# Both split parts of an operand in one tile, at chosen byte places

## The chip, the cores and the metric

The program runs on one core of a Trainium2 chip. The metric is the device time of one execution in microseconds, taken as the median of several runs; of the kernel before, three runs took 3246.57, 3247.99 and 3251.56 us. The page and the trace come from one profiled execution.

## The reference

Two stacks of layers work on 256 tokens of 1024 channels, in float32. The first block has two layers, each with a feed-forward, an attention of three kinds of heads and another feed-forward, whose norms are modulated by a vector c. The second has four layers, each with a mixer (a state-space model in layers 0 and 3, gated linear attention in 1, a gated delta rule in 2), a cross-attention to 256 memory tokens and a convolved feed-forward. Nearly all arithmetic is products with weights:

```python
def swiglu(h, w1, w3, w2):
    return (jax.nn.silu(h @ w1) * (h @ w3)) @ w2
...
x = x + 0.5 * g1 * swiglu(h, ffn_w1[layer, 0], ffn_w3[layer, 0], ffn_w2[layer, 0])
...
for i in range(DEPTH_2):
    hn = rmsnorm_2(x, ln_mix[i])
    mix = ...                      # mamba2_mixer, hgrn2_mixer or gated_deltanet_mixer
    x = x + mix.astype(x.dtype)
    x = x + memory_cross_attention(rmsnorm_2(x, ln_xattn[i]), rmsnorm_2(mem, ln_mem[i]), ...)
    x = x + conv_glu_ffn(rmsnorm_2(x, ln_ffn[i]), f_up[i], f_conv_w[i], f_conv_b[i], f_down[i])
return rmsnorm_2(x, final_norm)
```

D_FF is 2816. Products must come out at float32 precision.

## The kernel before

Activations lie channels on partitions, tokens along the free dimension. Each product is made of 128x128 blocks of weights as the stationary operand (`lhsT`, loaded by LDWEIGHTS) and 256 tokens of an activation as the one that streams past them (`rhs`). In a few places the roles are swapped, and weights stream past an activation: `wide_half`, and the memory's values in `kv`.

For precision both operands are split into two float32r parts that add up to them. `split` (L244 to L247) makes the high part with a copy on ACT and the low part with a subtraction on DVE, or, for a quarter of some slabs, on POOL. `mm3` (L312) then issues three matmuls: high by high, high by low and low by high. So one block costs three loads of weights and three matmuls of 256 columns.

Weights come from HBM as slabs of 128 x 2048 floats, 1 MB each, by `slab` (L249): SP loads a slab into one of three staging tiles `w`, then ACT and DVE write its parts into tiles `wh` and `wl`, of which there are three each, in two to four pieces. A slab serves 48 matmuls. An up projection (`up_block`) takes 8 chunks of the contraction by 3 matmuls for each of a slab's two column blocks; a down projection (`down_step`) 8 column blocks by 3 matmuls for each of two chunks, into four PSUM banks `acc`. A feed-forward (`glu`) goes over 11 groups of two up slabs and one down slab, the down product one group behind.

Tile names: `hh`/`hl` are a normed input's parts, `eh`/`el` those of a modulated norm with two shift columns behind each chunk (258 columns), `mh`/`ml` the memory's, `gh`/`gl` a feed-forward's inner values, `oh`/`ol`, `xoh`/`xol`, `myh`/`myl`, `hyh`/`hyl`, `gyh`/`gyl` outputs of the heads, `xk`, `xq`, `xp`, `xv` cross-attention's keys, queries, probabilities and values. Names in rows are written output, arrow, then what is read.

A scheduler orders each engine's instructions from the traced order and from what becomes free, and the tile framework sets the addresses within a partition: tiles follow each other as they are allocated, each beginning at a multiple of 32 bytes. In the built program they begin as follows, in bytes past a multiple of 512:

| tiles | before | after: the part's first byte |
|---|---|---|
| wh, wl (all three slots) | 32 | 0 |
| hh, hl | 64 | 192 |
| gh, gl of the first block (four tiles each) | 224 | 192 |
| gh, gl of the second block (two each) | 64 | 192 |
| xoh, xol | 64 | 192 |
| myh, myl, hyh, hyl | 320 | 192 |
| oh, ol, gyh, gyl | 256 | 192 |
| mh, ml (the memory's: first three layers, last) | 192, 64 | 192 or 448 |
| xph, xpl | 320 | 192 |
| xvh, xvl | 64 | 0 |
| xkh, xkl (stream past xq) | 64 | 0 |
| xqh, xql | 64 | 64 |
| eh, el (chunks of 1032 bytes: first chunk) | 352, 416 | 352, 416 |

Every chunk and column block of the weights and of h, g, o, m, xo, my and hy is a whole multiple of 512 bytes on, so that these places hold for each matmul on them; those of e move on by 8 bytes a chunk.

Of the kernel before, what the change touches and what calls it, by code (L numbers as in the profile page):

```python
# [8 lines left out]
F32 = mybir.dt.float32  # L9
F32R = mybir.dt.float32r  # L10
BF16 = mybir.dt.bfloat16
AF = mybir.ActivationFunctionType
OP = mybir.AluOpType
# [3 lines left out]
P = 128  # L17
T = 256
# [8 lines left out]
# ---------------------------------------------------------------- layout of small vectors  # L27
# [8 lines left out]
NMEM = 32  # L36
COFF, NCOL = {}, 0
# [7 lines left out]
def _consts():  # L45
# [11 lines left out]
        # sums from after a chunk's middle to each token, or negative from after the token to the middle  # L57
# [12 lines left out]
def _prepare(i):  # L70
    """Lays the inputs out: weights as slabs in the order they are used, vectors as columns."""
# [15 lines left out]
    def up(w, order=None):  # L87
        """[.., 1024, n] -> [.., n / 256, 128, 8, 256], column blocks of 128 in the order given."""
        lead, n = w.shape[:-2], w.shape[-1]
        w = w.reshape(-1, KC, P, n // P, P)  # L90
        if order is not None:
            w = w[:, :, :, order]
        nb = w.shape[3]
        w = w.reshape(-1, KC, P, nb // 2, 2 * P).transpose(0, 3, 2, 1, 4)
        return np.ascontiguousarray(w).reshape(*lead, nb // 2, P, KC * 2 * P)

    def down(w):
        """[.., k, 1024] -> [.., k / 256, 128, 2, 1024]."""
# [4 lines left out]
    def wide(w):  # L103
        """[.., 1024, n] -> [.., 2, 128, 4, n]: halves of the contraction."""
# [4 lines left out]
    def flat(w):  # L109
        """[.., 1024, n] -> [.., 128, 8 * n]."""  # L110
# [62 lines left out]
# ---------------------------------------------------------------- the program  # L173


class Normed:
    """The parts of something to be normed, and each token's factor, once it is worked out."""
# [10 lines left out]
class Net:  # L188
# [19 lines left out]
    # ---- small helpers  # L208

    @contextmanager  # L210
    def phase(self, name):
        """Tiles of a part of the program, given back at its end."""
# [10 lines left out]
    def t(self, shape, tag, dtype=F32, bufs=None, pool=None):  # L223
        pool = pool or self.tp
        k = {} if bufs is None else {"bufs": bufs}
        return pool.tile(list(shape), dtype, tag=tag, name=self.name(tag), **k)

# [16 lines left out]
    def split(self, src, hi, lo, engine=None):  # L244
        """src as a sum of two parts; returns the two instructions."""
# [3 lines left out]
    def slab(self, src, n=2048):  # L249
        """A slab of weights, as two parts that add up to it exactly."""  # L250
# [6 lines left out]
        hi = self.t([P, 2048], "wh", F32R, pool=self.sp)[:, :n]  # L257
        lo = self.t([P, 2048], "wl", F32R, pool=self.sp)[:, :n]
        m = n // self.pieces
        for k in range(0, n, m):  # L260
# [6 lines left out]
            if self.slabs == 2:  # L267
                # this slab's place is in use until the norm's input is there
# [16 lines left out]
    def link(self, ins):  # L285
        """In a chain the tensor engine keeps to the order that is traced."""
# [10 lines left out]
    def mm3(self, out, a, b, start, stop):  # L297
        """out += a.T @ b, both given as exact sums of two parts."""
# [7 lines left out]
    def rsqrt(self, out, src, scale):  # L306
        """out = (src * scale + eps) ** -0.5"""
# [3 lines left out]
    def newton(self, r, src, scale, n):  # L311
        """One step of Newton's for r = (src * scale + eps) ** -0.5"""  # L312
# [8 lines left out]
    def after(self, ins, before):  # L321
        """Issues ins behind an earlier instruction of its engine."""
# [7 lines left out]
    def act(self, out, src, func, **k):  # L330
        """An activation of one of the two tables in use: Silu's, or the one with both Ln and Exp. The scalar
        engine takes turns with them as they are traced."""
# [11 lines left out]
    # ---- start  # L344

    def load_cols(self):
        """All vectors but the memory's gains."""
# [33 lines left out]
    def load_consts(self):  # L381
        """Tables, and masks made from them."""
# [11 lines left out]
        # biases: queries on partitions (keys after the query), keys on partitions (keys from the query on)  # L394
# [9 lines left out]
    def start(self, kv):  # L404
        """The first of the memory's keys and values go along with the first modulation."""
# [17 lines left out]
    # ---- modulation  # L423

    def ada_slab(self, l, s):
        """256 columns of layer l's modulation: rows of its weights, over partitions, with silu(c)."""
# [30 lines left out]
    def need(self, l, chunk):  # L457
        """Has columns [chunk * 1024, ..) of layer l's modulation worked out by now."""
# [3 lines left out]
    def mod_cols(self, l, i):  # L462
        """(gain, shift) of the i-th norm of layer l."""
# [19 lines left out]
    # ---- norms  # L483

    def square_sums(self, b, x, s, engine=None, behind=None):
        """Adds the squares of x's pair of chunks b to the sums so far; the last give what is left to add up."""
# [29 lines left out]
    def rstd(self, parts, cols=False, r=None):  # L516
        """Each token's reciprocal root mean square, on all partitions; with cols also over tokens, behind."""
# [12 lines left out]
    def parts_of(self, x, gain, eh, el, sums=True, beside=None):  # L530
        """The parts of x * gain; and the sums of x's squares, but for the last addition."""
# [18 lines left out]
    def norm(self, gain, cols=False):  # L550
        """x normed, as the parts of x * gain, and a factor for each token, which goes to what comes of
        products with them."""
        e = [self.t([P, KC, T], "h" + k, F32R, pool=self.hp) for k in "hl"]
        return Normed(self, e, self.parts_of(self.x, gain, *e), cols)

    def norm_shift(self, gain, shift):
        """x normed and shifted: h, its parts; and for products that need not wait for the root mean
        square: e, x normed, with the parts of the shift behind each chunk."""
# [7 lines left out]
        h = [self.t([P, KC, T], "h" + k, F32R, pool=self.hp) for k in "hl"]  # L566
# [23 lines left out]
    def scale(self, out, ps, r):  # L590
        """out [128, n, T] = products with e, of a bank or a part of it, times r."""
# [5 lines left out]
    def project(self, src, n, tag, bufs=2, bank=None):  # L597
        """Two blocks of a projection of x normed: [128, 2, T]."""
# [7 lines left out]
    # ---- feed forward  # L606
# [5 lines left out]
    def down_step(self, acc, w, j, g, first, last, banks=range(4)):  # L612
        """acc += w[k-chunk j].T @ g"""
# [1506 lines left out]
```

## Time and profile before

| | us |
|---|---|
| median of three runs | 3247.99 |
| lowest, highest | 3246.57, 3251.56 |
| the profiled execution's own span | 3242.8 |
| PE busy (matmuls) | 3123.4 (96%) |
| PEld busy (loads of weights) | 3022.4 (93%) |
| DVE busy | 2406.3 (74%) |
| ACT busy | 1874.0 (58%) |
| POOL busy | 614.6 (19%) |
| mean DMA rate | 193 GB/s, 624.85 MB in all |

The span goes from the first instruction to the last; a run's time has some launch and end around it, here 5.2 us between the span and the median. A matmul's listed duration reaches from its start to the modelled end of its result and overlaps the next ones, so that a matmul of 256 columns is shown with some 280 ns although the next begins long before; the pace of a run of matmuls is read from their starts. The granted clock of TensorE is 0.989 of full speed on the mean.

### The profile page before, as it was taken

Reading aid. Unit: us, or ns where it says so; the run is one execution under the profiler, and the core shown is the slowest. Engines: PE = TensorE matmul, PEld = TensorE weight load, DVE = VectorE, ACT = ScalarE, POOL = GpSimd, SP = SyncE. Lnnn points to the kernel's source line nnn. Section 1 sums busy time; section 2 is a strip of 40 time slices with the busy share of each in tenths; the row PEclk is TensorE's granted clock in tenths of the full one; section 3 lists DMA queues with packets and bytes.
Section 4 is the critical chain, followed back from the end, with each engine's and each line's share of the span. In section 5 each row is a group of like instructions: output and inputs, shape, how many; then the busy total and the mean of one; then the engine's idle time right before and its main releaser. Section 6 shows DMA issues by size and latency. Waiting matters only on the chain. (4 is left out here: it accounts for less than half of the span.)

```text
span 3242.8 us, 63167 instructions
## 1 busy us (share of the span) xinstructions
PE 3123.4 (96%) x25866; PEld 3022.4 (93%) x25866; DVE 2406.3 (74%) x4122; ACT 1874.0 (58%) x3317; POOL 614.6 (19%) x522
## 2 busy tenths in 40 slices
PE   8999999999999999999999999998899999999998
PEld 8999889999988999889999999997799999889998
DVE  6877778777776857887767677688857766887765
ACT  5544566454466546775546655476466545776544
POOL 1100232010032102433001220036422000443100
PEclk9999999999999999999999999999999999999999
DMA  8978436758843655444554445544334555545453
GB/s 286 320 292 312 175 125 216 292 216 298 303 171 120 220 185 187 164 163 170 182 186 155 142 169 173 191 163 157 130 118 156 198 196 186 176 163 184 162 188 118
DMA packets 96754, 624.85 MB, mean 193 GB/s; under 512 B 10640, under 2 KB 14800, under 8 KB 25424
## 3 DMA queue, kind: packets, MB, share of 16 engines
q1 hardware_dynamic: 96464, 620.82, 54.7%
q8 instruction: 203, 3.33, 0.4%
q14 instruction: 87, 0.71, 0.1%
HBM read 607.08 MB, written 13.70 MB: 191 GB/s over the span
## 5 line engine op out<-in xcount | busy, mean ns | idle before, releaser
L246 ACT ACTIVATE wh<-w 128x512 fp32r<-128x512 f32 (+3 forms) x1392 | 1034.7, 788 | 773.7 <-issue 251.0
L247 DVE TENSOR_TENSOR wl<-w,wh 128x512 fp32r<-128x512 f32 (+3 forms) x1195 | 1140.9, 982 | 370.9 <-ACT wh L246 367.3
L283 PE MATMUL up<-hh,wh 128*128 128x256 f32 x4120 | 1158.2, 283 | 6.6 <-DVE gpr L593 6.2
L283 PE MATMUL up<-hh,wl 128*128 128x256 f32 x4120 | 1148.5, 281 | 1.3 <-DVE wl L247 1.0
L283 PE MATMUL up<-hl,wh 128*128 128x256 f32 x4120 | 1133.2, 282 | 4.1 <-DVE hl L247 4.1
L283 PEld LDWEIGHTS up<-hh,wh 128*128 128x128 f32 x4120 | 781.2, 190 | 15.9 <-ACT wh L246 7.0
L283 PEld LDWEIGHTS up<-hh,wl 128*128 128x128 f32 x4120 | 781.1, 190 | 2.6 <-DVE wl L247 2.5
L283 PEld LDWEIGHTS up<-hl,wh 128*128 128x128 f32 x4120 | 771.4, 190 | 7.1 <-DVE hl L247 5.1
L247 POOL TENSOR_TENSOR wl<-w,wh 128x512 fp32r<-128x512 f32 (+1 forms) x197 | 281.6, 1433 | 1395.9 <-ACT wh L246 1272.5
L283 PE MATMUL acc<-gl,wh 128*128 128x256 f32 x1408 | 391.7, 278 | 0.0
L283 PE MATMUL acc<-gh,wl 128*128 128x256 f32 x1408 | 391.5, 278 | 0.0
L283 PE MATMUL acc<-gh,wh 128*128 128x256 f32 x1408 | 391.4, 278 | 0.0
L283 PEld LDWEIGHTS acc<-gh,wl 128*128 128x128 f32 x1408 | 264.9, 188 | 0.0
L283 PEld LDWEIGHTS acc<-gh,wh 128*128 128x128 f32 x1408 | 264.9, 188 | 0.0
L283 PEld LDWEIGHTS acc<-gl,wh 128*128 128x128 f32 x1408 | 264.7, 188 | 0.1
L440 DVE SCALAR_TENSOR_TENSOR w<-w,silu_c 128x512 f32<-128x512 f32 x288 | 190.2, 711 | 55.5 <-DMA w<-ada 55.3
L505 POOL TENSOR_TENSOR nss<-nss,nsq 128x512 f32<-128x512 f32 x38 | 51.4, 1352 | 558.3 <-ACT nsq L492 557.0
L283 PE MATMUL up<-wh,hh 128*128 128x256 f32 (+1 forms) x352 | 106.2, 302 | 5.0 <-ACT hh L246 4.9
L283 PE MATMUL up<-wh,hl 128*128 128x256 f32 (+1 forms) x352 | 101.9, 290 | 1.2 <-DVE hl L247 1.1
L283 PE MATMUL up<-wl,hh 128*128 128x256 f32 (+1 forms) x352 | 101.4, 288 | 0.0
L335 ACT ACT_TABLE_LOAD x71 | 91.1, 1283 | 1.7 <-PEq L2110 0.7
L593 DVE TENSOR_TENSOR fgs<-up,nr 128x512 f32<-128x512 f32 x44 | 30.4, 691 | 80.1 <-PE up L283 80.1
(530 smaller groups left out, 5987.2 us busy)
## 6 DMA issues: line engine op xcount, KB each, us to landing
w<-w SPq DMA_DIRECT2D x132, 1024.0 KB, 5.3
w<-ada SPq DMA_DIRECT2D x72, 1024.0 KB, 5.1
w<-min SPq DMA_DIRECT2D x48, 1024.0 KB, 5.0
w<-fg SPq DMA_DIRECT2D x44, 1024.0 KB, 4.9
w<-fu SPq DMA_DIRECT2D x44, 1024.0 KB, 4.9
w<-fd SPq DMA_DIRECT2D x44, 1024.0 KB, 4.9
w<-gin SPq DMA_DIRECT2D x24, 1024.0 KB, 5.0
w<-xv SPq DMA_DIRECT2D x16, 1024.0 KB, 6.1
```

Source lines behind the costliest of these rows:

```text
L246: a = self.nc.scalar.activation(hi, src, AF.Copy)
L247: return a, (engine or self.nc.vector).tensor_tensor(lo, src, hi.bitcast(F32), op=OP.subtract)
L283: self.link(self.nc.tensor.matmul(out, lhsT=lhsT, rhs=rhs, start=start, stop=stop, skip_group_check=True))
L335: self.loaded = self.nc.scalar.preload_act_table_set(name)
L440: ins = nc.vector.scalar_tensor_tensor(c, c, 1.0, self.silu_c[:, z * 512 : z * 512 + 512], op0=OP.mult, op1=OP.mult, accum_out=sums[:, s % ...
L505: nc.gpsimd.tensor_tensor(s, s, q, op=OP.add)
L593: self.nc.vector.tensor_tensor(out, ps.rearrange("p (b t) -> p b t", b=n), r[:, :T].unsqueeze(1).to_broadcast([P, n, T]), op=OP.mult)
```

## The change

`parts` allocates both parts of an operand as one tile: `at` bytes, the high part, then the low part, the tile beginning at a multiple of 512 bytes. `at` is 192 by default and 0 for what is loaded as weights; for cross-attention's queries, loaded as weights against its keys, it is 64 with the keys at 0. The memory's parts stay two tiles, since there are two buffers of the high and one of the low part, each beginning at a multiple of 256 bytes and 192 behind it. `slab`, `norm`, `norm_shift`, `glu`, `attention_heads`, `mem_first`, `kv`, `cross`, `cross_head`, `mamba`, `hgrn` and `gdn_head` take their parts from it. Two tiles of the delta rule go: `q2` becomes a part of `at`, and the gates' `e` shares the tag of another tile. `eh` and `el` of `norm_shift` stay as they were. Comments are dropped. The core of the diff:

```diff
+AT = 192
...
-    def t(self, shape, tag, dtype=F32, bufs=None, pool=None):
+    def t(self, shape, tag, dtype=F32, bufs=None, pool=None, align=None):
         pool = pool or self.tp
         k = {} if bufs is None else {"bufs": bufs}
+        if align:
+            k["align_bytes"] = align
         return pool.tile(list(shape), dtype, tag=tag, name=self.name(tag), **k)
+
+    def parts(self, shape, tag, bufs=None, pool=None, at=AT):
+        n = int(np.prod(shape[1:]))
+        if isinstance(bufs, tuple):
+            out = [self.t([P, n + at // 4], tag + k, F32R, b, pool, 256)[:, at // 4 :] for k, b in zip("hl", bufs)]
+        else:
+            v = self.t([P, 2 * n + at // 4], tag + "p", F32R, bufs, pool, 512)[:, at // 4 : at // 4 + 2 * n]
+            out = [v[:, :n], v[:, n:]]
+        if len(shape) == 3:
+            out = [v.rearrange("p (a b) -> p a b", a=shape[1]) for v in out]
+        return out
...
-        hi = self.t([P, 2048], "wh", F32R, pool=self.sp)[:, :n]
-        lo = self.t([P, 2048], "wl", F32R, pool=self.sp)[:, :n]
+        hi, lo = (v[:, :n] for v in self.parts([P, 2048], "w", pool=self.sp, at=0))
...
-        e = [self.t([P, KC, T], "h" + k, F32R, pool=self.hp) for k in "hl"]
+        e = self.parts([P, KC, T], "h", pool=self.hp)
...
-            gs = [self.t([P, 512], "g" + x, F32R) for x in "hl"]
+            gs = self.parts([P, 512], "g")
...
-        oh = self.t([P, 8, T], "oh", F32R, bufs=1)
-        ol = self.t([P, 8, T], "ol", F32R, bufs=1)
+        oh, ol = self.parts([P, 8, T], "o", 1)
...
-        e = [self.t([P, KC, T], "m" + k, F32R, bufs=b) for k, b in (("h", 2), ("l", 1))]
+        e = self.parts([P, KC, T], "m", (2, 1))
...
-            hi, lo = (self.t([P, 2, T], tag + k, F32R) for k in "hl")
+            hi, lo = self.parts([P, 2, T], tag, at=0)
...
-        qh, ql = (self.t([P, 2, T], "xq" + k, F32R) for k in "hl")
+        qh, ql = self.parts([P, 2, T], "xq", at=64)
...
-        ph, pl = (self.t([P, 2, T], "xp" + k, F32R) for k in "hl")
+        ph, pl = self.parts([P, 2, T], "xp")
...
-            "yh": self.t([P, 16, T], "myh", F32R, bufs=1),
-            "yl": self.t([P, 16, T], "myl", F32R, bufs=1),
         }
+        d["yh"], d["yl"] = self.parts([P, 16, T], "my", 1)
...
-        yh = self.t([P, 8, T], "hyh", F32R, bufs=1)
-        yl = self.t([P, 8, T], "hyl", F32R, bufs=1)
+        yh, yl = self.parts([P, 8, T], "hyy", 1)
...
-        e = self.t([48, T], "gspe", bufs=1)[32:]
+        e = self.t([P, T], "gec", bufs=1)[32:48]
...
-        q2 = self.t([P, 4, 64], "gq2", bufs=4, pool=pool)
+        q2 = at[:, :, lo]
...
-        out[n] = [self.t([P, T], "gy" + k, F32R) for k in "hl"]
+        out[n] = self.parts([P, T], "gy")
```

The matmuls' order on PE is the same, high and low parts included. At the start of a down projection in the first block's feed-forward it stood like this before, with the waits in brackets:

```order
L283 MATMUL acc_1974<-gh_2104,wh_2306 128x256 [waits Activation_49]
L283 MATMUL acc_1974<-gl_2105,wh_2306 128x256
L283 MATMUL acc_1974<-gh_2104,wl_2307 128x256 [waits DVE_49]
L283 MATMUL acc_1974<-gh_2104,wh_2306 128x256
L283 MATMUL acc_1974<-gl_2105,wh_2306 128x256
L283 MATMUL acc_1974<-gh_2104,wl_2307 128x256
```

The same place now, where `gp` and `wp` are the tiles that hold both parts, so that rows on either part read alike and are counted together:

```order
L298 MATMUL acc_1946<-gp_2074,wp_2271 128x256 [waits Activation_49]
L298 MATMUL acc_1946<-gp_2074,wp_2271 128x256
L298 MATMUL acc_1946<-gp_2074,wp_2271 128x256 [waits DVE_49]
L298 MATMUL acc_1946<-gp_2074,wp_2271 128x256 x3
L298 MATMUL acc_1947<-gp_2074,wp_2271 128x256 x6
```

The waits stand at the same matmuls: the first waits for ACT's high parts, the third for DVE's low part of the weights.

On ACT some instructions change places with a neighbour. In the same feed-forward it had, before, the copies of a slab's two halves around the Silu (`s`) of the up product:

```order
L246 ACTIVATE wh_2306<-w_2304 128x1024 [waits DMAHW3_49,PE_49,Pool_49]
L246 ACTIVATE wh_2306<-w_2304 128x1024
L246 ACTIVATE wh_2371<-w_2369 128x1024 [waits DMAHW5_49,PE_49,Activation_49]
L339 ACTIVATE s_2183<-up_2192 128x512 [waits PE_49]
L246 ACTIVATE wh_2371<-w_2369 128x1024
L246 ACTIVATE wh_2428<-w_2426 128x1024 [waits DMAHW6_49,DVE_49,PE_49]
```

And now:

```order
L262 ACTIVATE wp_2271<-w_2269 128x1024 [waits DMAHW3_49,PE_49,Pool_49]
L262 ACTIVATE wp_2271<-w_2269 128x1024
L354 ACTIVATE s_2151<-up_2159 128x512 [waits PE_49]
L262 ACTIVATE wp_2335<-w_2333 128x1024 [waits DMAHW5_49,Activation_49]
L262 ACTIVATE wp_2335<-w_2333 128x1024
L262 ACTIVATE wp_2391<-w_2389 128x1024 [waits DMAHW6_49,DVE_49,PE_49]
```

The Silu stands ahead of both halves of the slab, where it stood between them.

## Rows read from the trace of the kernel before

**Rows 1.** Head of the page: span; busy time, share, instructions of each engine.
```profile
span 3242.8 us, 63167 instructions
...
PE 3123.4 (96%) x25866; PEld 3022.4 (93%) x25866; DVE 2406.3 (74%) x4122; ACT 1874.0 (58%) x3317; POOL 614.6 (19%) x522
```

**Rows 2.** Stretches: length, busy (instructions) PE, PEld, DVE, ACT, POOL; PEclk, DMA share, GB/s.
```profile
200.00:300.00 100.00, 100.00 (x866) 100.00 (x866) 76.20 (x144) 42.66 (x49) 0.00 (x0) 1.00 0.85 309
...
1600.00:1700.00 100.00, 100.00 (x859) 100.00 (x859) 67.31 (x84) 49.04 (x60) 0.00 (x0) 1.00 0.55 190
...
2200.00:2300.00 100.00, 83.78 (x605) 76.41 (x606) 87.84 (x142) 57.33 (x122) 72.77 (x84) 0.95 0.45 158
...
2800.00:2900.00 100.00, 92.31 (x726) 85.75 (x725) 85.28 (x146) 76.28 (x146) 42.95 (x37) 0.97 0.47 163
```

**Rows 3.** Page, instruction groups: names, shape, xcount, busy us, mean ns, idle before.
```profile
L283 PE MATMUL up<-hh,wh 128*128 128x256 f32 x4120 | 1158.2, 283 | 6.6 <-DVE gpr L593 6.2
...
L283 PE MATMUL acc<-gh,wh 128*128 128x256 f32 x1408 | 391.4, 278 | 0.0
...
L283 PE MATMUL up<-wh,hh 128*128 128x256 f32 (+1 forms) x352 | 106.2, 302 | 5.0 <-ACT hh L246 4.9
```

**Rows 4.** Timeline of PE, first-block down projections: start us, duration us, instruction.
```profile
333.10 0.28 PE L283 MATMUL acc<-gh,wh 128*128 128x256 f32 x1
...
344.00 0.28 PE L283 MATMUL acc<-eh,wh 128*128 128x258 f32 x1
```

**Rows 5.** Timeline of PE, second-block down projections, to the matmul behind them.
```profile
1724.66 0.28 PE L283 MATMUL acc<-gh,wh 128*128 128x256 f32 x1
...
1735.86 0.28 PE L283 MATMUL up<-hh,wh 128*128 128x256 f32 x1
```

**Rows 6.** Timeline of PE, up projections, to the matmul behind them.
```profile
1957.55 0.28 PE L283 MATMUL up<-hh,wh 128*128 128x256 f32 x1
...
1974.35 0.28 PE L283 MATMUL acc<-gh,wh 128*128 128x256 f32 x1
```

**Rows 7.** Timeline of PE, first and last of runs on m, o, my, xp.
```profile
67.21 0.28 PE L283 MATMUL up<-ml,wh 128*128 128x256 f32 x1
...
87.51 0.28 PE L283 MATMUL up<-mh,wl 128*128 128x256 f32 x1
...
1056.17 0.28 PE L283 MATMUL acc<-ol,wh 128*128 128x256 f32 x1
...
1064.57 0.28 PE L283 MATMUL acc<-eh,wh 128*128 128x258 f32 x1
...
1458.73 0.28 PE L283 MATMUL acc<-myl,wh 128*128 128x256 f32 x1
...
1475.29 0.28 PE L283 MATMUL acc<-myh,wl 128*128 128x256 f32 x1
...
3033.99 0.28 PE L283 MATMUL ms<-xph,xvh 128*128 128x256 f32 x1
...
3035.30 0.28 PE L283 MATMUL ms<-xph,xvl 128*128 128x256 f32 x1
```

**Rows 8.** Timeline of PE: modulated norm's products; swapped roles, weights streaming past m.
```profile
895.43 0.28 PE L283 MATMUL acc<-eh,wh 128*128 128x258 f32 x1
...
899.26 0.28 PE L283 MATMUL acc<-el,wh 128*128 128x258 f32 x1
...
2721.28 0.28 PE L283 MATMUL up<-wh,mh 128*128 128x256 f32 x1
...
2726.84 0.28 PE L283 MATMUL up<-wh,ml 128*128 128x256 f32 x1
```

**Rows 9.** Waits: who, for whom; us in total, times, longest us.
```profile
PE acc L283 <- DVE mm L1418: 18.3, 14, 1.9
...
ACT wh L246 <- PE acc L283: 209.4, 89, 6.5
...
SPq L256 <- DVE wl L247: 1947.5, 380, 19.3
```

More of the change, by code (lines that the diff above doesn't have):

```diff
@@ L565, in norm_shift @@
         e = Normed(self, (eh, el), self.parts_of(x, gain, eh, el, r is None))
-        h = [self.t([P, KC, T], "h" + k, F32R, pool=self.hp) for k in "hl"]
+        h = self.parts([P, KC, T], "h", pool=self.hp)
         def rest():
@@ L1105, in mem_first @@
         w = self.t([P, 2048], "w", pool=self.wp)
-        self.ready = hi, lo = [self.t([P, 2048], "w" + k, F32R, pool=self.sp) for k in "hl"]
+        self.ready = hi, lo = self.parts([P, 2048], "w", pool=self.sp, at=0)
         cut = [slice(512 * k, 512 * k + 512) for k in range(4)]
@@ L1157, in cross @@
         n = self.norm(self.col("ln_xattn", 8 * i, 8))
-        oh = self.t([P, 8, T], "xoh", F32R, bufs=1)
-        ol = self.t([P, 8, T], "xol", F32R, bufs=1)
+        oh, ol = self.parts([P, 8, T], "xo", 1)
         self.pieces = 4
```

## The prediction, on record before the change was timed

> **What bounds the kernel now.** I read the head of the page first: the program is busy on PE for 3123.4 of 3242.8 us, DVE for 74%, ACT for 58% [rows 1]. Because matmuls are pipelined and their ends modelled, that share alone could hide slack, so I then read the table of 100 us stretches [rows 2]: inside the feed-forward stages PE has 100.00 of 100 us and DVE no more than 76, and the emptiest one behind the start, 2200 to 2300, still has 83.78. The busy share is only the hint; what tells the real pace is the distance from one matmul's start to the next one's, and the timeline by instruction gives it. A 256-column matmul lasts 0.28 us in every row, yet the next one starts after 0.11 to 0.12 us; that distance, times the program's 23,496 matmuls on split parts, is over four fifths of the span. So the kernel is bound by how densely PE starts matmuls, not by waits: the longest wait of PE on one other place adds up to 18.3 us [rows 9].
>
> **The distance is not the same everywhere.** At the end of a first-block feed-forward 96 down-projection matmuls follow each other without a gap, from 333.10 to the next product's start at 344.00: 10.90 us, 113.5 ns each [rows 4]. The same helper, shape and order in a second-block feed-forward need 1724.66 to 1735.86 for 96 distances: 116.7 ns [rows 5]. An up projection needs 1957.55 to 1974.35 for 144: 116.7 ns [rows 6]. The granted clock is 1.00 of full speed (2.4 GHz) in stretches of either kind, 200 to 300 and 1600 to 1700 us [rows 2], so it is not the clock. Nor is it DVE, ACT or DMA beside it: the 200 to 300 stretch, with the faster down projections, is the one with more DVE work (76.20 against 67.31) and more DMA (309 against 190 GB/s). In 100 us it starts 866 matmuls, the other 859 [rows 2]; a third of its matmuls are down projections, and 2/3 x 116.7 + 1/3 x 113.5 = 115.6 ns gives 865. What is left is where the operands lie. By the table of places ahead, gh and gl lie at 224 past a multiple of 512 in the first block and at 64 in the second, against weights at 32 in both. Written as "streamed operand behind weights", that is 192 bytes against 32.
>
> The other places sort the same way. At 288 (my) 142 distances take 16.56 us, 116.6 ns, as at 32; at 224 (o) 71 take 8.40 us, 118.3; at 160 (m) 171 take 20.30 us, 118.7; at 256 (xp on xv) 11 take 1.31 us, 119.1 [rows 7]. Where roles are swapped and the weights stream past m, at -32, which is 224 past a multiple of 256, 47 take 5.56 us, 118.3 [rows 8], the same as o's 224 although both operands lie elsewhere. So I take the difference modulo 256 as what counts, and 192 is the only one seen at 113.5.
>
> **The change part by part.** It adds and removes no matmul, split or DMA of any size, and PE's order is the same instruction by instruction; what moves is every operand's address. After it, the difference is 192 modulo 256 for every product that streams h, g, o, my, xo, hy, gy, m or xp, and for xk on xq (0 against 64). The counts are three times those of the groups [rows 3]:
> - 32 or 288 behind now: up from h 12,360, half of the acc from g 2,112 (3 x 1408 / 2), and by the program 768 of h into acc, 768 xo, 768 my, 192 hy, 192 m: 17,160 x 3.1 ns (11.20 / 96 less 10.90 / 96) = 53.2 us.
> - 224 now, o and gy, 768 x (118.3 - 113.5) = 3.7 us. 160 now, 576 of m x 5.2 = 3.0 us. 0 or 256 now, xk and xp, 384 x 5.6 = 2.2 us.
> - g in the first block, 2,112, is at 192 already: nothing.
> - Swapped roles, weights streaming past h or m (960 and 768): now 118.3, afterwards 64 modulo 256, which no 256-column row shows. The nearest row is the modulated norm's 258-column stretch, whose differences run from 64 to 120: 32 distances in 3.83 us, 119.7, or 118.8 for 256 columns [rows 8]. I take 119: 1,728 x 0.7 = 1.2 us lost. The bounds are the fastest and the slowest pace seen, 113.5 (8 us gained) and 119.7 (2.4 us lost). The 258-column products themselves move from one unremarkable difference to another: nothing, within 672 x 5 ns = 3.4 us either way.
>
> The sum is 60.9 us. Two things come off. A matmul behind a wait does not start one distance after its predecessor; PE is busy 96% of the span, so I take 4%, 2.4 us. And in ten of the 33 stretches PE is busy under 96% (2200 to 2300 with 83.78 is the lowest behind the start, 2800 to 2900 with 92.31 the last [rows 2]): there a wait for another engine's chain can swallow what the matmuls ahead of it saved. These stretches hold many small products and, by my estimate, a quarter of the saving; half of that lost is 7 us, with bounds of nothing and 15. So 51 us go: the profiled span of 3242.8 becomes 3192, and the median of the runs, 5.2 us above that span, 3248.0 becomes 3197.
>
> One tile for both parts costs nothing on its own. The waits in the order show that the matmul on the high parts still waits for ACT and the one on the weights' low part for DVE, so no product waits for more than it did. A slot of the weights' ring now comes free when both halves are read; the last reads of the two halves are neighbours in each triple, 0.12 us apart, and three slots of 48 matmuls (5.6 us each) cover that. What sets ACT's pace there is mostly PE itself (209.4 us of ACT waiting for PE's slots, 89 times), and the weights' DMA waits for DVE to free the staging tile (1947.5 us, 380 times) [rows 9]: ACT, DVE and the DMAs follow PE, and can follow 3% faster. If that cover were gone, every 0.1 us per slab would cost some 40 us over the roughly 400 slabs. The silu that ACT now takes before a slab's halves instead of between them is off PE's path. gdn's q2 and e share tiles whose earlier readers are done.
>
> Here the Trainium skill speaks against the change. "TensorE: Matmul & The Clock Gate", in "Step-by-step: what each phase is for", says that PE has two independent SBUF read ports and that "Loading the next tile's weights doesn't steal SBUF read bandwidth from the running matmul." By that rule the place of the weights could not matter, and the sum would be 0. The trace does not agree: 113.5 against 116.7 ns between stretches that differ in the streamed tile's place [rows 4, 5].
>
> **The rivals.**
> 1. *Slower: the streamed operand's own place counts, and 192 is a bad one.* The m rows stream from 192 and take 118.7 [rows 7]. Then 17,160 matmuls pay 2.0 ns more (34 us), g of the first block 5.2 ns (11 us), o and m stay, and the time is about 3290. It decides as soon as the mean distance of the up projections rises above 116.7. For it: no row combines 192 with weights at 0. Against it: 64 and 320 agree to 0.1 ns, and 224 behind gives 118.3 from two different places [rows 6 to 8]. Chance 0.06.
> 2. *No change:* the 3 ns belong to something that goes with the first block's g and not with its place. For it: only g shows 113.5, and the skill's rule above. Against it: the first block's up projections run right beside g in the same stretch and fit 116.7, and second-block g, same code, does too. 3248, chance 0.05.
> 3. *Part is given back:* PE outruns the splits or the loads. In 200 to 300 us the DMAs already move 309 GB/s at a share of 0.85, and from 2200 to 2300 DVE is busy 87.84 of 100 [rows 2]; if the first 300 us save nothing (5 us) and the stretches with waits nothing either (another 8), and a tenth of the rest is lost at the slabs' starts, the time is 3215; with a fifth or more, 3220 to 3232. Chance 0.12.
> 4. *More than the sum:* all of it is credited and the swapped products come to 113.5 as well: 61 + 9 = 70 us, 3178. Multiples of 512 might also shorten 113.5 itself; no row here shows a shorter steady pace. The skill's page gives for 256 columns 256/2.4 + 2.5 = 109 ns ("Back-to-back issue gap"), an estimate by which another 4 ns x 21,000 = 90 us would lie below; this sentence enters no number here. Chance 0.07.
>
> **How the numbers follow.** My forecast, 3197, has 0.70, with its own range of 3183 (waits swallow nothing) to 3212. From 3178 (case 4) to 3232 (case 3's far end) the range holds that and nearly all of case 3 and half of case 4; what lies outside is the slower case, the unchanged one and the far side of case 4. A measurement of this kernel can tell about 0.2%, 6.5 us, from no change. Faster by more than that: cases 3, 4 and the forecast, 0.70 + 0.12 + 0.07 = 0.89; within it 0.05; slower 0.06.
>
> **What would show it.** In the profile after, a run of 96 down-projection matmuls should take 10.9 us in both blocks, and 144 up-projection matmuls 16.35 us instead of 16.80; the stretches in which PE is full should hold about 880 matmuls in 100 us instead of 859. Swapped products, weights streaming past h or m, should not improve. PE's waits for ACT wh or DVE wl should grow by no more than some 8 us together. The forecast is wrong if the distance falls but the span does not (case 3), or if the distance stays at 116.7 or rises for up projections (cases 2 and 1).

## The result and the profile after

Five runs of the changed kernel took 3222.64 to 3241.09 us, median 3230.92; five of the kernel before beside them 3246.57 to 3251.56, median 3249.81. The ratio is 0.995, with a 95% interval of 0.9937 to 0.9963: 19 us faster where the prediction had 51. The runs of the changed kernel lie 18 us apart, those of the kernel before 5 us. The profiled run is one of the longer ones, 3237.62 us.

The head of its page answers to [rows 1]:

```profile
span 3235.8 us, 63172 instructions
...
PE 3113.1 (96%) x25866; PEld 3009.9 (93%) x25866; DVE 2407.7 (74%) x4122; ACT 1871.9 (58%) x3317; POOL 616.2 (19%) x522
```

PE is as full as before. Stretches, for [rows 2] (columns as there):

```profile
200.00:300.00 100.00, 100.00 (x884) 100.00 (x884) 79.86 (x148) 45.27 (x51) 0.00 (x0) 1.00 0.87 321
600.00:700.00 100.00, 100.00 (x852) 100.00 (x851) 71.87 (x125) 44.11 (x52) 0.84 (x1) 1.00 0.76 283
1600.00:1700.00 100.00, 100.00 (x884) 100.00 (x884) 69.47 (x87) 51.10 (x63) 0.00 (x0) 1.00 0.57 195
2000.00:2100.00 100.00, 100.00 (x852) 100.00 (x851) 66.08 (x83) 47.72 (x59) 0.00 (x0) 1.00 0.54 184
2200.00:2300.00 100.00, 82.64 (x589) 74.67 (x587) 86.50 (x137) 58.64 (x122) 71.45 (x83) 0.91 0.42 149
```

The first four lie inside feed-forwards, PE is full in all of them and the granted clock is at its upper level (2.4 GHz). Two hold 884 matmuls, as the prediction wanted (880), and two hold 852, fewer than the 859 and 866 of before. The emptiest stretch behind the start, 2200 to 2300, has PE busy for 82.64 us, not for more than before (83.78), at a clock of 0.91. The timeline says the same for 96 down products each; answering to [rows 4, 5], the start, the length of the whole run and its count, and then what starts behind it:

```profile
333.21 11.04 PE L298 MATMUL acc<-gp,wp 128*128 128x256 f32 x96
344.09 1.12 PE L298 MATMUL acc<-eh,wp 128*128 128x258 f32 x8
...
696.11 11.47 PE L298 MATMUL acc<-gp,wp 128*128 128x256 f32 x96
707.41 0.77 PE L298 MATMUL acc<-eh,wp 128*128 128x258 f32 x5
...
1730.04 11.47 PE L298 MATMUL acc<-gp,wp 128*128 128x256 f32 x96
1741.35 0.87 PE L298 MATMUL up<-hp,wp 128*128 128x256 f32 x6
```

From start to start 10.88, 11.30 and 11.31 us: 113.3, 117.7 and 117.8 ns a matmul, with g at 192 and weights at 0 every time. So one place has two paces, and 117.8 is worse than the 116.7 it replaced. Products in swapped roles show the same pair, the first and the last row of 48 steps each for [rows 8]:

```profile
2653.67 0.39 PE L298 MATMUL up<-wp,mh 128*128 128x256 f32 x2
...
2659.11 1.11 PE L298 MATMUL up<-hp,wp 128*128 128x256 f32 x8
...
2676.07 0.40 PE L298 MATMUL up<-wp,mh 128*128 128x256 f32 x2
...
2681.73 0.85 PE L298 MATMUL up<-hp,wp 128*128 128x256 f32 x6
```

5.44 us (113.3 ns) and 5.66 us (117.9 ns), against 118.3 before.

For one number per kernel I matched the matmuls of two traces in their order and took the difference of each start-to-start distance. *Pace* is the sum where both distances are under 130 ns and the matmul has 256 columns (some 22,000 of 25,866), *rest* everything else: waits, and what runs at the lower clock (1.2 GHz). In this profile pace gives -27.6 us and rest +20.6.

**The clue stood in the trace of before.** Of its 41 unbroken runs at difference 192, 40 came straight from up products at 32 and ran at 113.3 ns. One did not; four rows of the timeline of before around it:

```profile
884.21 0.28 PE L283 MATMUL acc<-gh,wh 128*128 128x256 f32 x1
...
889.66 0.28 PE L283 MATMUL acc<-gh,wh 128*128 128x256 f32 x1
...
890.01 0.28 PE L283 MATMUL acc<-gh,wl 128*128 128x256 f32 x1
...
895.43 0.28 PE L283 MATMUL acc<-eh,wh 128*128 128x258 f32 x1
```

48 distances in the first 5.45 us are 113.5 ns; then there is a break of 0.23 us, and the 46 distances from 890.01 take 5.42 us, 117.8 ns, on the same tiles.

The difference 32 has two paces in that trace as well: of 220 unbroken runs of 21 or more up products on h, 20 ran at 117.8 ns and not at 116.7. One of them, 60 distances behind a break, to the down product that ends it:

```profile
536.16 0.28 PE L283 MATMUL up<-hh,wh 128*128 128x256 f32 x1
...
543.23 0.28 PE L283 MATMUL acc<-gh,wh 128*128 128x256 f32 x1
```

That is 7.07 us, 117.8 ns.

### The profile page after: what moved, and what is told of

Same layout as the page of the kernel before. It is cut to its first block, busy times and chain, and to the rows that moved or that the text cites. A ratio compares the mean times of both kernels' runs of the same rounds, so it can differ in the third digit from the quotient of the medians.

```text
span 3235.8 us, 63172 instructions
## 1 busy us (share of the span) xinstructions
PE 3113.1 (96%) x25866; PEld 3009.9 (93%) x25866; DVE 2407.7 (74%) x4122; ACT 1871.9 (58%) x3317; POOL 616.2 (19%) x522
## 5 line engine op out<-in xcount | busy, mean ns | idle before, releaser
L298 PE MATMUL up<-hp,wp 128*128 128x256 f32 x12360 | 1495.5, 282 | 14.9 <-DVE gpr L608 8.1
L298 PEld LDWEIGHTS up<-hp,wp 128*128 128x128 f32 x12360 | 1464.2, 191 | 28.3 <-issue 10.4
L262 ACT ACTIVATE wp<-w 128x512 fp32r<-128x512 f32 (+3 forms) x1392 | 1034.6, 787 | 699.7 <-PE acc L298 227.6
L263 DVE TENSOR_TENSOR wp<-w,wp 128x512 fp32r<-128x512 f32 (+3 forms) x1195 | 1139.9, 984 | 387.4 <-ACT wp L262 375.8
L263 POOL TENSOR_TENSOR wp<-w,wp 128x512 fp32r<-128x512 f32 (+1 forms) x197 | 282.7, 1438 | 1389.1 <-ACT wp L262 1284.5
L298 PE MATMUL acc<-gp,wp 128*128 128x256 f32 x4224 | 502.2, 279 | 0.0
L298 PEld LDWEIGHTS acc<-gp,wp 128*128 128x128 f32 x4224 | 494.7, 189 | 0.2
L298 PE MATMUL up<-wp,hp 128*128 128x256 f32 (+1 forms) x1056 | 145.1, 293 | 6.0 <-ACT hp L262 4.3
L298 PEld LDWEIGHTS up<-wp,hp 128*128 128x128 f32 x1056 | 134.4, 196 | 12.7 <-ACT hp L262 5.9
L298 PE MATMUL acc<-hp,wp 128*128 128x256 f32 x768 | 95.0, 280 | 0.0
```

The lines of the kernel that those rows point to most:

```text
L262: a = self.nc.scalar.activation(hi, src, AF.Copy)
L263: return a, (engine or self.nc.vector).tensor_tensor(lo, src, hi.bitcast(F32), op=OP.subtract)
L298: self.link(self.nc.tensor.matmul(out, lhsT=lhsT, rhs=rhs, start=start, stop=stop, skip_group_check=True))
```

## Theories

A: at 192 two paces hold themselves; the start behind each interruption picks one, and it lasts until the next interruption. B: the slower one is brought from outside (DMA, other engines), at certain places of the program. C: 192 bytes as a place is at fault, not as a difference. In the first profile after there are 182 unbroken runs of 21 or more matmuls on streams at 192, counted so that products in swapped roles end a run: 133 are fast and 49 slow, none changes inside, and the longest has some 1,580; no address separates fast from slow. That is for A.

## First experiments: draw, place, a start from 32, other places

**again**: the changed kernel, unchanged. 

> The changed kernel once more, nothing altered. In its first profile the products at difference 192 run either at 113.3 or at 117.8 ns from start to start, each for hundreds of matmuls, and no address separates the two. Theory A (a state chosen anew wherever the stream of matmuls is interrupted): other stretches than in the first profile are fast and slow; the share of the slow ones, and with it the span, is another, somewhere from 3220 to 3240 us. Theory B (something fixed in the program: an address, a neighbour, an order): the same stretches are slow as before, 550 to 900, 1100 to 1250 and 1950 to 2150 us among them, and the span is within 3 us of 3235.8.

3221.06 us; pace -40.4, rest +16.8. Stretches in feed-forwards of this profile:

```profile
600.00:700.00 100.00, 100.00 (x883) 100.00 (x882) 74.95 (x132) 49.89 (x66) 5.32 (x4) 1.00 0.81 291
1120.00:1220.00 100.00, 100.00 (x885) 100.00 (x884) 51.27 (x49) 44.25 (x50) 0.00 (x0) 1.00 0.58 199
2000.00:2100.00 100.00, 100.00 (x851) 100.00 (x851) 65.73 (x81) 48.24 (x60) 0.00 (x0) 1.00 0.54 185
3050.00:3150.00 100.00, 100.00 (x852) 100.00 (x851) 67.50 (x84) 48.22 (x60) 0.00 (x0) 1.00 0.53 185
```

600 to 700 was slow in the first profile (852) and is fast here; two of eight feed-forwards are slow, where four were. The same program in the same place has either pace: B falls as far as it means places in the program. (The feed-forward at 2000 is slow in all three profiles of the changed kernel; three draws can't tell whether it leans that way.)

**shift32**: everything 32 bytes on, differences kept.

```diff
-AT = 192                                   # weights' tiles begin at 0, xq at=64
+AT = 224                                   # weights' tiles with align=32, so at 32; xq at=96
```

> All places 32 bytes on: weights at 32 past a multiple of 512, what streams past them at 224, the very places at which the first block's inner values were before; the difference stays 192. Theory A: again both paces, 113.3 and 117.8, in a mixture, with a span of 3215 to 3245 us. Theory C (the place itself: 32 and 224 are good, 0 and 192 are not): 113.3 nearly throughout, under 5% of the matmuls over 116 ns, span some 3190 us.

3222.36 us; pace -30.9, rest +9.0. Up products average 115.2 ns, with the same pair 113.3 and 117.8 and three feed-forwards slow. The same two paces come back at other places with the same difference: C falls.

**kick**: the first of eleven g groups of each feed-forward at 32.

```diff
-            gs = self.parts([P, 512], "g")
+            gs = self.parts([P, 512], "g", at=AT if s else 32, room=AT)
```

(`room` only keeps the tile's size.) 

> The changed kernel with one edit: the first of the eleven groups of inner values in each of the eight feed-forwards lies 32 behind the weights instead of 192, so that one down product of 48 matmuls runs at the old difference before the long uninterrupted rest. In the profile of before, all 40 runs at difference 192 that came straight from products at 32 ran at 113.3, and the only one that came after an interruption ran at 117.8. Theory A with a handover (a pace of 116.7 leads into 113.3): behind that product the rest of every feed-forward runs at 113.3, some 11,000 matmuls; the median falls to 3200 to 3212 us and the runs differ less than the changed kernel's 3223 to 3241. Theory A without one (each start is a draw): some feed-forwards stay at 117.8 and the median stays at 3225 to 3235.

3220.73 us (ratio to before 0.9915, 0.9902 to 0.9929), pace -41.7: faster than the changed kernel, not as fast as expected. Six of eight feed-forwards ran at 113.3 behind the kick, two at 117.8. The 48 steps at 32 have two patterns of their own with one mean, 113, 116, 118, 120 ns or 117, 117, 116 ns: all six behind the first turned out fast, both behind the second slow. Most of this was settled ahead of the kick: in five of the six the up products before it already ran at 113.3, in the two at 117.8, and one alone (at 2523) went from 117.8 to 113.3. So 48 matmuls at 32 mostly hand on the pace that they meet. They don't decide it either: in before, the down products at 183.2 us followed the second pattern and were fast.

**sweep1**: other differences, read per product.

```diff
+h at=208, g at=176, xo at=240, my at=128, o at=112, hyy at=144, gy at=16
```

> Other differences, to see whether any has one pace only: inputs h 208 behind the weights, inner values g 176, cross-attention's output 240, the state-space mixer's output 128, the attention's 112, linear attention's 144, the delta rule's 16. Theory A says nothing of their sizes; from the differences seen (0: 119.4, 32: 116.7, 160: 118.5, 224: 118.3) I expect 116 to 120 ns for each, and a span of 3240 to 3275 us. A theory by which the pace changes evenly with the difference puts 176 and 208 between 113.5 and 118.5, at about 116.

3273.68 us. Mean distances: h 118.6, g 119.2, xo 117.2, my 118.7, hyy 118.1, gy 117.7. But o at 112 settled at 113.3 ns in 12 of 12 runs, within a dozen steps, also behind interruptions. That led to the next runs.

## Second: 112, alone and as a start; the places of before in one tile

**at112**:

```diff
-AT = 192
+AT = 112
-        qh, ql = self.parts([P, 2, T], "xq", at=64)
+        qh, ql = self.parts([P, 2, T], "xq", at=144)
```

> Everything that streams past the weights lies 112 bytes behind a multiple of 256 instead of 192 (xq moved so that xk on it has 112 too); nothing else changes. In the run with eight places the 12 stretches of o at 112 all settled at 113.3 ns within a dozen steps, whatever came before them. Theory A (at 192 there are two paces that hold themselves, and the start behind each interruption picks one; at 112 only the fast one holds itself): no stretch at 117.8, mean distance 113.4 to 113.8 ns instead of 115.4, so 21,000 x 1.8 ns = 38 us less than the 3231 of the changed kernel, about 3190 to 3200; swapped products, now at 144, cost up to 4 us. Rival C (the slower pace comes from something outside the matmuls, at changing times, and o's few products were lucky): stretches at 117.8 remain, 3220 to 3240.

3209.78 us, ratio to before 0.9872 (0.9856 to 0.9889). All 187 unbroken runs of 21 or more steps ended at 113.3; straight products average 113.8 ns. Two stretches:

```profile
600.00:700.00 100.00, 100.00 (x884) 100.00 (x884) 75.60 (x130) 46.94 (x55) 1.37 (x1) 1.00 0.82 301
...
2000.00:2100.00 100.00, 100.00 (x885) 100.00 (x884) 68.94 (x86) 49.07 (x61) 0.00 (x0) 1.00 0.55 192
```

Pace gives -53.9 us, nearly what the prediction's terms add up to (60.9), so the slow pace needs no outside cause (the expectation calls that cause C; above it is B): A holds so far. The time is 10 us above the range expected, because rest gives +24.7. Two side results: swapped products, now at 144, take 120.0 ns, and xk on xq 119.5 although its difference is 112 too, with weights at 144. The difference alone is not the whole rule; whether it is the weights' place, no multiple of 32 here, no run shows.

**g112**: only g at 112, all else at 192.

```diff
-            gs = self.parts([P, 512], "g")
+            gs = self.parts([P, 512], "g", at=112)
```

> Only g of the feed-forwards lies at 112, all else at 192. Theory A with the state handed over from product to product: from the first g group of each feed-forward on, g and h both run at 113.3 to its end (8 of 8 feed-forwards), starts behind interruptions elsewhere stay mixed; about 3205 to 3215. Rival (each product picks its pace anew, or the pace comes from outside): g at 113.3, but h's products after it still 117.8 in two to four of the feed-forwards.

3216.6 us; pace -47.4, rest +19.6. The timeline shows the handover:

```profile
2705.49 11.47 PE L298 MATMUL up<-hp,wp 128*128 128x256 f32 x96
2716.80 11.08 PE L298 MATMUL acc<-gp,wp 128*128 128x256 f32 x96
2727.72 4.71 PE L298 MATMUL up<-hp,wp 128*128 128x256 f32 x40
2732.26 0.59 PE L298 MATMUL ms<-nss,ones 128*128 128x256 f32 x2
```

h at 192 runs at 117.8 ns (11.31 / 96), then g at 112 settles (10.92 / 96 = 113.8), and h, still at 192, goes on at 113.5 (4.54 / 40). Wherever h follows g directly it is fast, in eight of eight feed-forwards. The pace is a state that is handed on. The slow h in the first row doesn't follow a g: between them stand 48 products in swapped roles, for the memory's values, which only the seventh feed-forward has; there these take 117.8 ns and h behind them too, four times in a row. More on that under kick112.

**at32**: one tile and aligned weights, streams at the 32 that most had.

```diff
-AT = 192                                   # xq at=64
+AT = 32                                    # xq at=224
```

> One tile for both parts and the aligned weights as in the changed kernel, but everything that streams lies at 32, the difference that most products had before. If the places alone decide: 116.7 ns everywhere, first-block g loses the 113.3 that it had (2,112 x 3.3 = 7 us), o, m, gy, xk, xp gain some 6 us, so 3245 to 3255, the time of the kernel before. If the single tile or the aligned weights save something by themselves: 3240 or less.

3255.73 us, ratio 1.0018 (1.0007 to 1.0030). One tile and alignment save nothing by themselves; the gain is all in the difference. Not expected: whole feed-forwards, three of eight, run at the second pace of 32. 851 matmuls in 100 us are 117.8 ns, 860 are 116.7:

```profile
200.00:300.00 100.00, 100.00 (x851) 100.00 (x850) 77.56 (x145) 42.89 (x49) 0.00 (x0) 1.00 0.85 312
1600.00:1700.00 100.00, 100.00 (x860) 100.00 (x859) 66.77 (x84) 48.24 (x61) 0.00 (x0) 1.00 0.54 189
```

**sweep2**: seven more places.

```diff
+h at=48, g at=80, xo at=64, my at=116, o at=104, hyy at=120, gy at=96
```

> A table of further differences in one run: h at 48, g at 80, xo at 64, my at 116, o at 104, hy at 120, gy at 96. Theory A expects other steady paces between 113.3 and 120 ns per difference and for some of them two; nothing under 113.3. h and g carry most products, so the time is 3230 to 3275 unless one of them is at 113.3.

3271.16 us. Means: h 118.3, g 118.5, xo 116.8, my 121.4, o 123.8, hyy 120.7, gy 119.7. Nothing steady under 113.3. The mean of xo hides two paces: at 64, 8 of its 24 runs went at 113.3 and 16 at 117.8, the same pair as at 192.

## Third: the best version, a smaller start, and 192 behind 32

**mix**: 112 for what only streams, 192 for what also serves as weights or has short runs.

```diff
-AT = 192
+AT = 112
+        h, e = self.norm_shift(*self.mod_cols(l, 1), at=192)        # attention
+        n = self.norm(self.col("ln_mix", 8 * i, 8), True, at=192)   # hgrn
+        e = self.parts([P, KC, T], "m", (2, 1), at=192)
+        out[n] = self.parts([P, T], "gy", at=192)                   # xq stays at 64
```

> Streams at 112, but what also serves as weights in swapped products, or has short runs (h of the attention and of hgrn, m, gy, xk on xq), stays at 192. Theory A, from the two profiles of 192 and 112: swapped products 116.5 ns instead of 119.2 (1,930 x 2.7 = 5.2 us less than with 112 everywhere), xk on xq and gy 1.5 us less, straight products of m and those two h 1.5 us more: 5 us under the 3209.8 of 112 everywhere, 3205. If the swapped products follow something else: 3210 or more.

3203.21 us, ratio to before 0.9867 (0.9847 to 0.9887): the best median, 28 us under the changed kernel. Swapped products take 117.0 ns where they took 120.0 with 112 everywhere; pace -58.5 us, rest +17.1.

**kick112**: the kick with 112 in the place of 32.

```diff
-            gs = self.parts([P, 512], "g")
+            gs = self.parts([P, 512], "g", at=AT if s else 112, room=AT)
```

> As the changed kernel, all at 192, but the first of the eleven g groups of each feed-forward (48 matmuls of some 1,400) at 112. If the state is handed over and 112 always leaves the fast one: all 8 feed-forwards at 113.3 from there on, where the same 48 matmuls at 32 left 6 of 8 fast; mixed paces elsewhere as before; 3207 to 3217. If 112 only runs fast itself: feed-forwards mixed as in the changed kernel, 3222 to 3241.

3208.58 us, 0.9873 (0.9858 to 0.9888); pace -54.0, rest +22.9. All eight feed-forwards are fast behind the kick, the seventh until its first swapped products; here the one that was slow in all three profiles of the changed kernel:

```profile
2000.00:2100.00 100.00, 100.00 (x885) 100.00 (x884) 69.03 (x86) 50.97 (x64) 0.00 (x0) 1.00 0.55 194
```

In four of the eight, this one among them, the up products ahead of the kick ran at 117.8, and all four turned. 48 matmuls at another place, of some 1,400, set the pace of the others: the state is handed on, and 112 sets it, where the kick at 32 turned one of three.

An interruption isn't the only thing that changes the pace. In the seventh feed-forward, without any break, it turns at each group of swapped products (weights streaming past m, difference 64):

```profile
2624.55 5.60 PE L298 MATMUL acc<-gp,wp 128*128 128x256 f32 x48
2629.99 0.39 PE L298 MATMUL up<-wp,mh 128*128 128x256 f32 x2
...
2635.43 11.47 PE L298 MATMUL up<-hp,wp 128*128 128x256 f32 x96
2646.74 5.82 PE L298 MATMUL acc<-gp,wp 128*128 128x256 f32 x48
...
2658.05 11.05 PE L298 MATMUL up<-hp,wp 128*128 128x256 f32 x96
```

g and the 48 swapped products behind it take 5.44 us each, 113.3 ns; h and g behind those 11.31 us for 96 and 5.66 for 48, 117.8 ns; behind the next swapped products h is fast again. The swapped products have the pace of what runs ahead of them, and what follows has the other one: 24 times of 24 where the difference ahead and behind is 192, in the profiles of the changed kernel (three), shift32, kick and kick112. Theory A holds with this added. Why they turn it is open.

**g192**: h at 32, g at 192 in every block.

```diff
-AT = 192                                   # xq at=64
+AT = 32                                    # xq at=224
-            gs = self.parts([P, 512], "g")
+            gs = self.parts([P, 512], "g", at=192)
```

> All that streams at 32, only g of the feed-forwards at 192, in every block: every feed-forward as the first block's were in the kernel before. Theory A: a start at 192 straight behind h at 32 ends in the fast pace nearly always, so g 113.3 to 113.7 in all eight feed-forwards and h 116.7; 4,224 x 3.5 ns = 15 us under the 3256 of 32 everywhere, 3236 to 3246. Rival (192's pace is picked by chance at every start): g mixed, mean 115.4.

g 113.6 to 114.0 ns and, from the first g on, h 116.7 in every feed-forward, as expected: the row that the prediction took its 113.5 from is reproduced, by a start behind 32. The time, 3249.52 us, missed the range: pace is 17 us better than in the profile of at32, rest 17 us worse (one run, at a mean clock of 0.985).

**at112b**: 112 everywhere, profiled again. 

> 112 everywhere once more, unchanged, for a second profile. Theory A: again no stretch of 20 or more at 117.8, mean distance of straight products 113.8; what differs from the first profile is the granted clock's low stretches between 2150 and 2450 us. 3205 to 3215.

3215.57 us; pace -53.9 again and every feed-forward at 113.3; rest +25.2.

## Last: what is given back

**before2** and **before3**: the kernel before, unchanged. 

> The kernel before, unchanged, profiled again. Its first profile shows a granted clock under 1.00 in stretches that add up to (1 - clock) x 50 us = 30.5 us; the profiles of the changed kernel show 47.5 and 45. If how often the clock falls is drawn anew in each execution, this profile may show anything from 27 to 48 (what the profiles of twelve kernels so far show); if it goes with the pace of the matmuls, 28 to 34. The pace itself: the same as in the first profile product by product, 116.5 ns on average, since 32 and 192 behind 32 held in every stretch.

> As the one before it: lost clock 28 to 34 us if it goes with the pace, anywhere from 27 to 48 if it is drawn; pace 116.5 ns.

3245.93 and 3250.98 us; pace -0.2 and +1.3, rest +1.7 and +5.3 against the first profile. But before has a draw too, at 32: in before3 its last feed-forward ran at 117.8, here against the first profile:

```profile
3100.00:3200.00 100.00, 100.00 (x860) 100.00 (x859) 66.70 (x83) 48.58 (x60) 0.00 (x0) 1.00 0.55 190
3100.00:3200.00 100.00, 100.00 (x851) 100.00 (x851) 66.24 (x83) 49.06 (x60) 0.00 (x0) 1.00 0.54 187
```

It is one feed-forward of 24 in three profiles, and costs less, since 117.8 and 116.7 lie closer together. The clock lost, (1 - granted clock) x 50 us summed over stretches, is 27.5 and 29.0 us (first profile 30.5; the changed kernel's first two 47.5 and 45).

**again2**: the changed kernel a third time. 

> The changed kernel a third time. Theory A: another set of slow feed-forwards than (543, 1101, 1975) and (1950, 3043); mean pace between 114.3 and 115.6 ns, and a time between 3215 and 3241 that follows it: about 21.5 us per ns of pace, of which a quarter is given back in waits, and about 0.8 us per us of lost clock above 30.5.

3238.94 us; pace -22.5, rest +17.3, lost clock 39. Another set of feed-forwards is slow (those at 600, 1120, 1600 and 2000); the straight mean is 115.65 ns, just outside what was expected.

**mix2**: the best version again. 

> The version with 112 for the streams and 192 for what also serves as weights, a second profile: pace 113.85 again; lost clock 28 to 34 us if it goes with idle stretches rather than with the pace, 40 or more if it goes with a fast pace; the time follows: 3200 to 3203 with the former, 3207 to 3215 with the latter.

3204.33 us, pace -59.8, rest +19.9, lost clock 35.5, between the two cases. So even with a pace near the forecast's a third comes back. Rest has two parts, told apart by whether a distance reaches into a stretch at the lower clock (1.2 GHz) in either of the two traces:

| profile | pace, us | rest at the lower clock | rest elsewhere |
|---|---|---|---|
| at32 | +7.9 | +0.3 | -2.8 |
| changed kernel, first | -27.6 | +16.5 | +4.1 |
| again | -40.4 | +13.7 | +3.1 |
| again2 | -22.5 | +5.8 | +11.5 |
| at112 | -53.9 | +11.3 | +13.4 |
| mix | -58.5 | +0.7 | +16.4 |
| mix2 | -59.8 | +3.6 | +16.3 |

In the first two profiles of the changed kernel most of what is given back is given back at the lower clock; in mix nearly all of it elsewhere. Elsewhere it is waits, mainly: all of PE's idle time adds up to 111.2 us in before, 107.5 in at32, 114.4 in the changed kernel, 125.0 in mix and 126.5 in mix2. The largest single wait, 18.3 us in before [rows 9], is this in at32, in the changed kernel and in mix (total, times, longest):

```profile
PE acc L298 <- DVE mm L1430: 21.8, 14, 2.2
```

```profile
PE acc L298 <- DVE mm L1430: 22.7, 14, 2.6
```

```profile
PE acc L298 <- DVE mm L1430: 26.0, 14, 2.9
```

at32, no faster than before, has most of this wait's growth in the changed kernel already, so that growth isn't the price of the pace. The growth in mix fits PE reaching another engine's chain earlier in the mixers, but no run shows that wait by wait. The clock differs most in the delta rule's stage, here one part of it in before and in the changed kernel:

```profile
2350.00:2400.00 50.00, 47.46 (x573) 44.60 (x572) 29.07 (x66) 32.87 (x90) 8.86 (x9) 1.00 0.29 96
```

```profile
2350.00:2400.00 50.00, 48.08 (x545) 44.55 (x535) 27.03 (x68) 29.15 (x78) 6.70 (x7) 0.86 0.21 71
```

From 2300 to 2400 rest alone is +7.1 us. 32 runs of the kernel before have mean clocks of 0.987 to 0.991 (mean 0.9891), the five each of changed and mix 0.984 to 0.989 (0.9862, 0.9866), a mean difference of 0.0029 of 3232 us, some 9 us. The pace alone doesn't explain it: at32, no faster than before, has a mean of 0.9869 over ten runs. Inside one kernel the time goes with it (mix 3199.89 us at 0.989, 3214.66 at 0.984). What lowers the clock stays open.

## Why the prediction was wrong

- **The bound and the source of the gain were right**: PE is full, the pace depends on where the two operands lie against each other, and one tile costs nothing (at32, within 0.3%).
- **The step that failed: "17,160 x 3.1 ns = 53.2 us"**, with the other terms at 113.5. It took the 113.5 ns of [rows 4] as the pace of difference 192. The runs show it to be one of two paces there, held from a start to the next interruption or to swapped products; [rows 4] was fast because it began straight behind products at 32 (g192 repeats that in eight of eight feed-forwards). Three profiles of the changed kernel give 27.6, 40.4 and 22.5 us where the terms add up to 60.9. Where every start ends fast, 53.9 (at112) to 59.8 (mix2) came: the size was right for that case. The check that was left out: do all runs at 192 in the trace have this pace? One of 41 did not, at 890.01 us, right beside [rows 8], and neither did 20 of the 220 runs of up products at 32, which the sum takes at 116.7 throughout.
- **Swapped products "1.2 us lost"**: gained. 64 modulo 256 has the same two paces, on average 116.7 ns against 118.9, some 3.8 us for 1,728; 119 was taken from 258-column products whose difference moves on by 8 bytes a chunk. (The trace has 576 of these, not 672; the term stood at nothing.)
- **"2.4 and 7 us come off" left out the clock.** Rest is +16.8 to +20.6 in the three profiles. Of that, 4.1, 3.1 and 11.5 us lie outside the lower clock's stretches, within the bounds that the waits were given; 16.5, 13.7 and 5.8 lie in them, a term that the sum put at nothing. With a pace near the forecast's, in mix, 16.4 us come back outside them, near the upper bound of the waits, 15, plus 2.4.
- **Rival 3's time was right (3215 to 3232), its reason was not**: the first profile has 33 us less pace than forecast and 11 us more given back, and what came back is mostly the clock (16.5 of 20.6), not PE outrunning the splits or the loads. That the time fell there is luck. The slower rival by a bad 192 was half right in kind: 117.8 is a bad pace of 192, but of the draw, not of the place. Rival 4's 109 ns was reached in no run; the fastest steady pace is 113.3 ns.
- **The signs named in advance**: about 880 matmuls in full stretches came, in some feed-forwards; "in both blocks" was the clause that showed the failure, 10.88 us in one and 11.31 in the other.

## What to carry to other kernels

A pace read from one stage belongs to the conditions of its start too: before multiplying it by a count, list every run with the same operands and look for the one that differs. A layout whose every run settles at the same pace beats one whose best pace is equal. A wide spread between runs asks for more than one profile, but isn't itself a sign of a drawn pace: the runs of mix, whose pace was the same in both profiles, lie 15 us apart, with the clock. Part of what a faster matmul saves is given back in waits, here 16 of 58 us at the best pace, and a clock that is granted less can take as much again.

## What the hardware showed unexpectedly

The distance of 256-column float32r matmuls on weights at 0 goes by the streamed operand's byte place modulo 256: at 112 every run of 21 or more steps settles at 113.3 ns within a dozen steps, whatever came before; 192 gives either 113.3 or 117.8, and so does 64; 32 either 116.7 or 117.8; 240 and 16 about 117 to 118; 48, 80, 128, 144, 176 and 208 about 118 to 119; 96, 116 and 120 between 119.7 and 121.4. A pace outlives a change of operands without a break (g112), and 48 matmuls can set it for 1,300 (kick112). 48 products in swapped roles, at 64, between products at 192 turn the pace of these into the other one, 24 times of 24. The Trainium skill, "TensorE: Matmul & The Clock Gate", "Step-by-step: what each phase is for", lets loads of weights leave the streaming matmul's reading alone; by that alone the two operands' places against each other could not matter, and these runs show that they do. Whether it is the loads that get in the way, no run here shows. Why 112 leaves one state and 192 two is open.
